# Attention of a second block: probabilities divided before the transposes, values stationary on halves of TensorE's columns

## The chip, the cores and the metric

The kernel runs on one core of a Trainium2 chip. The metric is the device time of one execution in microseconds (us). The time before is the median of three runs.

## The reference, cut to what matters

The program computes two transformer blocks on 256 tokens of width 1024; all is f32. The change lies in the second block, which has three attentions, A, B and C, that read one normalised input h:

```python
qk = qk_norm_g[layer]
a_q = _rms(a_q.reshape(bsz, seq, A_HEADS, HEAD_DIM), qk[0])      # 8 heads of 64, one key/value head
y_a = _dsa_attention(a_q, a_k, a_v, i_q, i_k, i_w, rel_a) @ w_branch_a[layer]
y_b = _nsa_attention(b_q, ..., b_gates, ...) @ w_branch_b[layer]  # 8 heads, 2 key/value heads
y_c = _dilated_attention(c_q, c_k, c_v, rel_c) @ w_branch_c[layer]  # 3 groups of 4 heads
x = x + (g[:, :, 0] * y_a + g[:, :, 1] * y_b + g[:, :, 2] * y_c) @ w_out[layer]
```

Each is a softmax over the keys, p = e / sum(e), and then o = p @ v. A keeps the 64 best keys per query. B adds three results under gates: over 15 compressed keys, over selected blocks and over a window,

```python
o = gb[..., 0:1] * oc + gb[..., 1:2] * osel + gb[..., 2:3] * ow
```

C has three groups of heads; their outputs are weighted by a softmax over the groups' log sums, which is one softmax over the three groups' logits together. With 256 tokens the selected blocks and windows of B and C cover all earlier keys that their masks leave.

## The kernel before, in words

Tokens go in two tiles t of 128. In tile t the keys 0 to 128 (t + 1) count, so t = 0 has one key tile kt and t = 1 has two. The weight products of the program (projections, gates, branches; `mm3`, lines 78 to 80) split both operands into a high and a low part (hi by ScalarE, line 70; lo by VectorE, line 71) and run three fp32r matmuls. The products inside the attentions, other than the scores, are plain f32 matmuls.

One call of `attend` (A and B) handles four heads that share keys and values. `pair_scores` gives the scores of two heads at a time into an "s" bank; `logits` adds bias and mask and finds the row minimum (the scores are negated) on VectorE; `weigh` takes the exponential on ScalarE in place in `lg` with the row sum into `mx`; then, for each key tile, four transposes by TensorE into a "tp" bank (line 1095) and one copy to `pT` by VectorE (line 1096). The values follow head by head (line 1099): the transposed weights of one head (128 keys x 128 queries) are stationary, the 64 columns of values move, and the output, queries on partitions, lands in another "tp" bank:

```python
for i, (c, v) in enumerate(vs):
    for kt in range(t + 1):
        pe.matmul(po[:, c:c + 64], pT[kt][:, i, :], v(kt), ...)
```

Behind that VectorE multiplies the output by one over the row sum (in B also by the gate, and adds it to `oB`): lines 1230, 1338 and 1340, in C line 1375. `split_oT` transposes the finished output (128 queries x 512, in C x 256) in tiles of 128 columns by TensorE (line 1120) and splits it into `oTh` (ScalarE, line 1123) and `oTl` (VectorE, line 1124), which the branch's product needs. A has two attends per token tile, B the compressed part (lines 1311 to 1328) and four attends, C two rounds `jp`, each with two heads of three groups (`weigh` with `joint`).

PSUM has eight banks: four "mm" (projections, gates, branches), two "tp" (transposes and outputs), two "s" (scores). `lg` has two buffers, `mx` and `pT` three.

Instructions are ordered at build time by the tile framework's planner: it runs the program in a model of the engines, and each engine takes, of what is ready, what comes first in the program; a buffer is given out when its first writer is ready. So work that stands later in the program fills gaps: while A's attention runs, the projection `P1` (line 1233); beside B's and C's, `gates(1)` and `gates(2)`. `behind(ins)` queues an instruction behind another one of the same engine, without a wait for its end. Weight units (`wunit`) go through three buffers in fixed turn, so a unit is loaded and split when the third before it has been used up.

Line 1258 is the one place before that puts 64 stationary columns alternately on the two halves of PE's columns (`X[par * 64:(par + 1) * 64, ...]`): 16 f32 matmuls with 64 moving columns.

Of the kernel before, what the change touches and what calls it, by code (L numbers as in the profile page):

```python
# [10 lines left out]
F32 = mybir.dt.float32  # L11
F32R = mybir.dt.float32r
AF = mybir.ActivationFunctionType
ALU = mybir.AluOpType
# [17 lines left out]
def tile_net(ctx: ExitStack, tc: tile.TileContext, I: dict, out: bass.AP):  # L32
# [9 lines left out]
    def bank():  # L42
        return ps.tile([128, 512], F32, tag="mm", name="mm", bufs=4)

    def tbank():
        return ps.tile([128, 512], F32, tag="tp", name="tp", bufs=2)
# [914 lines left out]
    with tc.tile_pool(name="b2", bufs=1, reuse_waits="tile") as b2:  # L961
# [43 lines left out]
        def t512(nm):  # L1005
            return b2.tile([128, 512], F32, tag="t512", name=nm, bufs=3)
# [69 lines left out]
            for j, i in enumerate(at):  # L1076
                ve.tensor_tensor_reduce(lg[:, i, :nk], S[:, j, :], W[j], 1.0, 3e38, ALU.add, ALU.min, mx[:, i:i + 1])

        def weigh(t, n, lg, mx, joint, po, vs):


            nk = 128 * (t + 1)
            if joint:
                ve.tensor_reduce(mx[:, 4:5], mx[:, 0:n], axis=AX.X, op=ALU.min)
                se.activation(lg[:, 0:n, :nk], lg[:, 0:n, :nk], AF.Exp, bias=mx[:, 4:5], scale=-1.0,
                              accum_out=mx[:, 12:13])
            else:
                for i in range(n):
                    se.activation(lg[:, i, :nk], lg[:, i, :nk], AF.Exp, bias=mx[:, i:i + 1], scale=-1.0,
                                  accum_out=mx[:, 12 + i:13 + i])  # L1090
            pT = [b2.tile([128, 4, 128], F32, tag="pT", name="pT", bufs=3) for _ in range(t + 1)]
            for kt in range(t + 1):
                b = tbank()
                for i in range(n):
                    pe.transpose(b[:, i * 128:(i + 1) * 128], lg[:, i, kt * 128:(kt + 1) * 128], ident)  # L1095
                ve.tensor_copy(pT[kt][:, :n, :], b[:, :n * 128].rearrange("p (n c) -> p n c", n=n))
            for i, (c, v) in enumerate(vs):
                for kt in range(t + 1):
                    pe.matmul(po[:, c:c + 64], pT[kt][:, i, :], v(kt),  # L1099
                              start=kt == 0 and (not joint or i == 0), stop=kt == t and (not joint or i == n - 1))  # L1100
            return mx[:, 12:13] if joint else mx[:, 12:12 + n]

        def soft_tiles():
            return (b2.tile([128, 4, 256], F32, tag="lg", name="lg", bufs=2),
                    b2.tile([128, 16], F32, tag="mx", name="mx", bufs=3))

        def attend(t, q, g, kz, W, po, v):


            nk = 128 * (t + 1)  # L1110
            lg, mx = soft_tiles()
            Ss = [pair_scores(t, q, 2 * g + i, kz, nk) for i in range(2)]
            for i in range(2):
                logits(nk, Ss[i], [W(2 * i), W(2 * i + 1)], lg, mx, (2 * i, 2 * i + 1))
            return weigh(t, 4, lg, mx, False, po, [(64 * i, v) for i in range(4)])

        def split_oT(o_t, nb, oTh, oTl, t):
            b = tbank()
            for i in range(nb):
                pe.transpose(b[:, i * 128:(i + 1) * 128], o_t[:, i * 128:(i + 1) * 128], ident)  # L1120
            bv = b[:, :nb * 128].rearrange("p (n c) -> p n c", n=nb)
            tk = slice(t * 128, (t + 1) * 128)
            se.copy(oTh[:, :nb, tk], bv)
            ve.tensor_sub(oTl[:, :nb, tk], bv, oTh[:, :nb, tk].bitcast(F32))
# [90 lines left out]
        oTh, oTl = oT_tiles()  # L1215
        for t in range(2):
            nk = 128 * (t + 1)
            oA = t512("oA")
            for hg in range(2):
                if t == 0:  # L1220
                    Wm = t2k("W0").rearrange("p (h k) -> p h k", h=4)
                    wv = WA[hg][:, :, 128:256]
                else:
                    Wm = wv = WA[hg]
                ve.tensor_add(Wm, wv, madd[t][:, None, :nk].to_broadcast([128, 4, nk]))
                po = tbank()
                den = attend(t, qT, hg, 1, lambda i: Wm[:, i, :nk], po, lambda kt: vA[:, kt, :])
                rden = b2.tile([128, 4], F32, tag="rden", name="rden", bufs=2)
                ve.reciprocal(rden, den)
                ve.tensor_mul(oA[:, hg * 256:(hg + 1) * 256].rearrange("p (h c) -> p h c", c=64),  # L1230
                              po[:, :256].rearrange("p (h c) -> p h c", c=64), rden[:, :, None].to_broadcast([128, 4, 64]))
            split_oT(oA, 4, oTh, oTl, t)
        gA_ = gates(0, *seq["ix"])
        P1 = project(1476, 384)
        branch(0, I["w_branch_a_2"][0], 4, oTh, oTl, gA_)
# [66 lines left out]
        for t in range(2):  # L1302
            tk = slice(t * 128, (t + 1) * 128)
            nk = 128 * (t + 1)
            oB = b2.tile([128, 512], F32, tag="so", name="oB", bufs=2).rearrange("p (h c) -> p h c", c=64)
            co = b2.tile([128, 5, 8], F32, tag="co", name="co", bufs=2)

            Sc = sbank()[:, 0:128].rearrange("p (r h n) -> p r h n", r=4, h=2)
            for pr in range(4):
                for i, (a, c) in enumerate(((0, 0), (1, 0), (0, 1))):  # L1310
                    pe.matmul(Sc[:, pr], qT[:, pr, a, tk], kcZ[:, pr // 2, c], start=i == 0, stop=i == 2)
            pcb = b2.tile([128, 8, 16], F32, tag="pc", name="pc", bufs=1)
            ve.tensor_add(pcb, Sc.rearrange("p r h n -> p (r h) n"), nmask[:, t, None, 0:16].to_broadcast([128, 8, 16]))
            ve.tensor_reduce(co[:, 0, :], pcb, axis=AX.X, op=ALU.min)
            ve.tensor_sub(pcb, pcb, co[:, 0, :, None].to_broadcast([128, 8, 16]))
            se.activation(pcb, pcb, AF.Exp, scale=-1.0)
            ve.tensor_reduce(co[:, 1, :], pcb, axis=AX.X, op=ALU.add)
            ve.tensor_scalar(co[:, 1, :], co[:, 1, :], 1e-30, None, op0=ALU.max)
            ve.reciprocal(co[:, 2, :], co[:, 1, :])
            ve.scalar_tensor_tensor(co[:, 2, :], bgv[:, t, :, 0], nmask[:, t, 16:17], co[:, 2, :],  # L1320
                                    op0=ALU.mult, op1=ALU.mult)
            b = tbank()
            pe.transpose(b[:, 0:128], pcb.rearrange("p h n -> p (h n)"), ident)
            pcT = b2.tile([128, 128], F32, tag="pcT", name="pcT", bufs=1)
            se.copy(pcT, b[:, 0:128])
            po = tbank()
            pe.matmul(po, pcT, vbd.rearrange("p h c -> p (h c)"), start=True, stop=True)
            ve.tensor_mul(oB, po.rearrange("p (h c) -> p h c", c=64), co[:, 2, :, None].to_broadcast([128, 8, 64]))
            for br in range(2):
                for g in range(2):  # L1330
                    po = tbank()
                    den = attend(t, qT, g, 2 * br + g, lambda i: WB[g][:, i, 256 - nk:256], po,
                                 lambda kt: vB[:, kt, 2 * br + g, :])
                    cc = co[:, 3 + br, 4 * g:4 * g + 4]
                    ve.reciprocal(cc, den)
                    ve.tensor_mul(cc, cc, bgv[:, t, 4 * g:4 * g + 4, 1 + br])
                    tmp = t512("ot")[:, :256].rearrange("p (h c) -> p h c", c=64)
                    ve.tensor_mul(tmp, po[:, :256].rearrange("p (h c) -> p h c", c=64),
                                  cc[:, :, None].to_broadcast([128, 4, 64]))
                    ve.tensor_add(oB[:, 4 * g:4 * g + 4, :], oB[:, 4 * g:4 * g + 4, :], tmp)  # L1340
            split_oT(oB.rearrange("p h c -> p (h c)"), 4, oTh, oTl, t)
        gB_ = gates(1)
        branch(1, I["w_branch_b_2"][0], 4, oTh, oTl, gB_)

# [14 lines left out]
        oTh, oTl = oT_tiles()  # L1359
        for t in range(2):  # L1360
            nk = 128 * (t + 1)
            oC = t512("oC")
            for jp in range(2):
                soft = [soft_tiles() for _ in range(2)]
                for g in range(3):
                    S = pair_scores(t, qT, 2 * g + jp, 2 * g + jp, nk)
                    for i in range(2):
                        logits(nk, S[:, i:i + 1], [WC[g][:, 2 * jp + i, 256 - nk:256]], *soft[i], (g,))
                for i in range(2):
                    j = 2 * jp + i  # L1370
                    po = tbank()
                    den = weigh(t, 3, *soft[i], True, po, [(0, lambda kt, h=4 * g + j: vC[:, kt, h, :]) for g in range(3)])
                    rden = b2.tile([128, 4], F32, tag="rden", name="rden", bufs=2)
                    ve.reciprocal(rden[:, 0:1], den)
                    ve.tensor_scalar_mul(oC[:, j * 64:(j + 1) * 64], po[:, 0:64], rden[:, 0:1])
            split_oT(oC, 2, oTh, oTl, t)
        gC_ = gates(2)
        yT = h_tiles()
        branch(2, I["w_branch_c_2"][0], 2, oTh, oTl, gC_, yT)
# [107 lines left out]
```

## Time and profile before

| | us |
|---|---|
| median of 3 runs (1150.12 to 1151.07) | 1150.55 |
| the profiled execution | 1151.18 |
| its span, first to last instruction | 1149.4 |
| PE busy (share of the span) | 1131.6 (98%) |
| VectorE (DVE) busy | 831.6 (72%) |
| ScalarE (ACT) busy | 575.3 (50%) |

PE is TensorE's matmuls, PEld its loads of stationary operands, which overlap with them. A busy instruction is one that is somewhere between its start and its modelled end; matmuls are pipelined, so busy time counts latency too. The stages are, from the span's start: A's attention 702.9 to 727.1 us, B's 778.9 to 818.4, C's 884.6 to 920.9. TensorE's granted clock is 1.00 (2.4 GHz) in all three.

### The profile page before, as it was taken

What the parts mean: (1) busy time and instruction counts of PE and PEld (TensorE: products, weight loads), DVE (VectorE), ACT (ScalarE), POOL (GpSimd) and SP (SyncE); (2) the same over time, 40 slices, a digit from 0 to 9 for tenths busy, and PEclk for the clock granted to TensorE, in tenths of its full rate; (3) what the DMA queues carried; (4) which work ended last, traced back from release to release, by engine and by line L of the source; (5) the groups of instructions that cost most, each with busy time, mean ns of one, the idle gap of its engine ahead of it and who ended that gap; (6) DMA issues with size and microseconds to landing.
All of it is one profiled execution on the core that took longest, in us unless ns stands there. A gap on an engine that the chain in (4) does not pass through costs nothing.

```text
span 1149.4 us, 19941 instructions
## 1 busy us (share of the span) xinstructions
PE 1131.6 (98%) x8007; PEld 1040.1 (90%) x8007; DVE 831.6 (72%) x1547; ACT 575.3 (50%) x1017; POOL 84.1 (7%) x154
## 2 busy tenths in 40 slices
PE   8999999999999999999999999999999999999998
PEld 6989988889999877999988889989999989999986
DVE  5798896889878778766754789788788674655541
ACT  5654444475444436654544665355356356545430
POOL 0111110101121111100000111000100000000000
PEclk9999999999999999999999999999999999999999
DMA  9985554749997993867664283750556254664630
GB/s 310 302 265 160 184 185 141 219 153 336 313 329 284 354 315 106 267 204 254 212 213 137 83 257 114 202 175 28 147 166 221 87 178 139 220 202 166 218 111 37
DMA packets 149098, 229.69 MB, mean 200 GB/s; under 512 B 5708, under 2 KB 121051, under 8 KB 149006
## 3 DMA queue, kind: packets, MB, share of 16 engines
q1 hardware_dynamic: 133986, 176.54, 47.1%
q0 software_dynamic: 14672, 50.63, 13.3%
q8 instruction: 63, 1.03, 0.4%
q10 hardware_dynamic: 348, 1.26, 0.3%
q14 instruction: 29, 0.24, 0.1%
HBM read 226.36 MB, written 2.04 MB: 199 GB/s over the span
## 4 chain that ended last, share of the span: by engine, by line
PE 90%; DVE 7%; ACT 2%; issue 1%; DMA 0%; SPq 0%; DVEq 0%; ACTq 0%
PE mm L80 25%; PE mm L78 25%; PE mm L79 25%; PE tp L1099 2%; DVE wlo L71 2%; PE s L1071 2%; PE s L712 2%; PE tp L736 1%; PE tp L1095 1%; PE s L138 1%; PE s L543 1%; PE tp L723 1%; PE s L542 1%; PE mm L890 1%; PE s L145 1%
## 5 line engine op out<-in xcount | busy, mean ns | idle before, releaser
L71 DVE TENSOR_TENSOR wlo<-raw,whi 128x1024 fp32r<-128x1024 f32 (+2 forms) x316 | 370.7, 1193 | 136.3 <-ACT whi L70 135.8
L70 ACT CAST whi<-raw 128x1024 fp32r<-128x1024 f32 (+2 forms) x316 | 314.6, 1029 | 231.0 <-PE mm L79 95.6
L78 PE MATMUL mm<-hTh,whi 128*128 128x256 f32 x1056 | 297.9, 282 | 0.0
L80 PE MATMUL mm<-hTh,wlo 128*128 128x256 f32 x1056 | 297.6, 282 | 0.0
L79 PE MATMUL mm<-hTl,whi 128*128 128x256 f32 x1056 | 297.1, 281 | 0.0
L79 PEld LDWEIGHTS mm<-hTl,whi 128*128 128x128 f32 x1056 | 199.0, 188 | 0.3
L78 PEld LDWEIGHTS mm<-hTh,whi 128*128 128x128 f32 x1056 | 198.9, 188 | 0.3
L80 PEld LDWEIGHTS mm<-hTh,wlo 128*128 128x128 f32 x1056 | 198.9, 188 | 0.1
L78 PE MATMUL mm<-whi,hTh 128*128 128x256 f32 (+4 forms) x592 | 186.0, 315 | 2.6 <-DVE hTh L336 2.2
L80 PE MATMUL mm<-whi,hTl 128*128 128x256 f32 (+4 forms) x592 | 185.3, 314 | 0.4 <-DVE hTl L337 0.4
L79 PE MATMUL mm<-wlo,hTh 128*128 128x256 f32 (+4 forms) x592 | 184.3, 312 | 0.3 <-DVE wlo L71 0.2
L78 PEld LDWEIGHTS mm<-whi,hTh 128*128 128x128 f32 x592 | 112.2, 189 | 8.8 <-DVE hTh L336 3.1
L80 PEld LDWEIGHTS mm<-whi,hTl 128*128 128x128 f32 x592 | 111.4, 189 | 5.4 <-DVE hTl L337 1.1
L79 PEld LDWEIGHTS mm<-wlo,hTh 128*128 128x128 f32 x592 | 111.9, 189 | 4.3 <-DVE wlo L71 0.7
L132 DVE SCALAR_TENSOR_TENSOR acc<-mraw,csil,acc 128x1024 f32<-128x1024 f32 x80 | 102.1, 1280 | 6.4 <-DMA mraw<-in_w_mod_dram 3.4
L79 PE MATMUL mm<-wlo,hid 128*128 128x512 f32 x264 | 104.2, 395 | 0.0
L78 PE MATMUL mm<-whi,hid 128*128 128x512 f32 x264 | 104.1, 394 | 0.0
L80 PE MATMUL mm<-whi,hid 128*128 128x512 f32 x264 | 103.6, 392 | 0.0
L131 POOL DMA_DIRECT2D mraw<-in_w_mod_dram x80 | 42.8, 535 | 343.9 <-DVE acc L132 235.1
L80 PEld LDWEIGHTS mm<-whi,hid 128*128 128x128 f32 x264 | 49.6, 188 | 12.0 <-issue 1.0
L79 PEld LDWEIGHTS mm<-wlo,hid 128*128 128x128 f32 x264 | 49.6, 188 | 11.6 <-issue 1.0
L78 PEld LDWEIGHTS mm<-whi,hid 128*128 128x128 f32 x264 | 49.6, 188 | 10.9 <-ACT whi L70 0.5
(331 smaller groups left out, 1568.5 us busy)
## 6 DMA issues: line engine op xcount, KB each, us to landing
raw<-in_ffn_w_in_dram SPq DMA_DIRECT2D x44, 1024.0 KB, 7.9
mraw<-in_w_mod_dram POOLq DMA_DIRECT2D x80, 512.0 KB, 5.1
raw<-in_ffn_w_out_dram SPq DMA_DIRECT2D x22, 1024.0 KB, 4.9
raw<-in_w_ffn_in_dram SPq DMA_DIRECT2D x22, 1024.0 KB, 5.2
raw<-in_w_in_dram SPq DMA_DIRECT2D x16, 1024.0 KB, 7.4
raw<-in_w_ffn_out_dram SPq DMA_DIRECT2D x11, 1024.0 KB, 5.0
raw<-in_w_in_dram SPq DMA_DIRECT2D x14, 768.0 KB, 4.4
raw<-in_attn_w_qkv_dram SPq DMA_DIRECT2D x9, 1024.0 KB, 8.9
```

Of the source, the lines that this page charges most:

```text
L70: se.copy(hv[:, sl], raw[:, sl])
L71: seq["sub"] = ve.tensor_sub(lv[:, sl], raw[:, sl], hv[:, sl].bitcast(F32)).ins
L78: pe.matmul(o, lh, rh, start=first, stop=False, **kw)
L79: pe.matmul(o, lh, rl, start=False, stop=False, **kw)
L80: return pe.matmul(o, ll, rh, start=False, stop=last, **kw).ins
L131: gp.dma_start(raw, wv[:, k, g * 1024:(g + 1) * 1024])
L132: ve.scalar_tensor_tensor(acc, raw, csil[:, k, 0:1], acc, op0=ALU.mult, op1=ALU.add)
L138: pe.matmul(b[:, j:j + 1], acc[:, j * 128:(j + 1) * 128], ones[:, 0:1], start=True, stop=True)
L145: mods["mm"] = pe.matmul(b, ones, acc[:, n * 512:(n + 1) * 512], start=True, stop=True).ins
L712: last = pe.matmul(Sm[m], q[p, h, tk], k[p, h, :], start=i == 0, stop=i == 2).ins,
L1071: pe.matmul(S, q[:, pr, a, tk], KZ[:, kz, b, :, :nk], start=i == 0, stop=i == 2)
L1099: pe.matmul(po[:, c:c + 64], pT[kt][:, i, :], v(kt), start=kt == 0 and (not joint or i == 0), stop=kt == t and (not joint or i == n - 1))
```

## The change

The exponentials are divided by their row sum (in B multiplied by the gate as well) on ScalarE, in place in `lg`, ahead of the transposes; in the compressed part VectorE does it on `pcb`. The values then become the stationary operand, 64 columns, and the transposed weights move: two heads side by side (256 columns) for one half of the output's partitions, the two other heads for the other half. The output comes out transposed, and everything that belongs to one token tile is summed in one "mm" bank `O`: in B the compressed part and all four attends. `split_oT` reads `O` directly. The division, the addition and the transposes of the outputs go away. The matmuls on halves are chained by `behind`, so that they stay in the order in which they are written. In `weights_T` the heads are laid out so that heads 0 and 2 stand side by side, then 1 and 3.

```diff
-            for i, (c, v) in enumerate(vs):
-                for kt in range(t + 1):
-                    pe.matmul(po[:, c:c + 64], pT[kt][:, i, :], v(kt), ...)
+        def weights_T(t, kt, n, lg):
+            b = tbank()
+            for i in range(n):
+                j = i % 2 * 2 + i // 2 if n == 4 else i
+                pe.transpose(b[:, j * 128:(j + 1) * 128], lg[:, i, kt * 128:(kt + 1) * 128], ident)
+            pT = b2.tile([128, 4, 128], F32, tag="pT", name="pT", bufs=3)
+            ve.tensor_copy(pT[:, :n, :], b[:, :n * 128].rearrange("p (n c) -> p n c", n=n))
+            return pT
+
+        def halves(O, c, first, last, vps):
+            for half, (v, w) in enumerate(vps):
+                with behind(*seq.get("halves", ())):
+                    i = pe.matmul(O[half * 64:(half + 1) * 64, c], v, w, start=first, stop=last, skip_group_check=True)
+                seq["halves"] = i.ins,
 ...
+            for i in range(4):                                     # attend, behind the exponentials
+                se.activation(lg[:, i, :nk], lg[:, i, :nk], AF.Exp, bias=mx[:, i:i + 1], scale=-1.0, ...)
+            ve.reciprocal(mx[:, 8:12], mx[:, 12:16])
+            if gate is not None:
+                ve.tensor_mul(mx[:, 8:12], mx[:, 8:12], gate)
+            for i in range(4):
+                se.activation(lg[:, i, :nk], lg[:, i, :nk], AF.Copy, scale=mx[:, 8 + i:9 + i])
+            pT = [weights_T(t, kt, 4, lg) for kt in range(t + 1)]
+            for kt in range(t + 1):
+                halves(O, slice(g * 256, (g + 1) * 256), first and kt == 0, last and kt == t,
+                       [(v(kt), pT[kt][:, 2 * i:2 * i + 2, :]) for i in range(2)])
 ...
-            for i in range(nb):                                    # split_oT
-                pe.transpose(b[:, i * 128:(i + 1) * 128], o_t[:, i * 128:(i + 1) * 128], ident)
 ...
+            ve.tensor_mul(pcb, pcb, co[:, 2, :, None].to_broadcast([128, 8, 16]))     # B, compressed part
-            pe.matmul(po, pcT, vbd.rearrange("p h c -> p (h c)"), start=True, stop=True)
-            ve.tensor_mul(oB, po..., co[:, 2, :, None].to_broadcast([128, 8, 64]))
+            for pr in range(4):
+                pe.matmul(O[:, pr * 128:(pr + 1) * 128], vbd[:, 2 * pr:2 * pr + 2, :]..., pcT, ...)
 ...
+                for lg, mx in soft:                                # C
+                    ve.tensor_reduce(mx[:, 4:5], mx[:, 0:3], axis=AX.X, op=ALU.min)
+                    se.activation(lg[:, 0:3, :nk], lg[:, 0:3, :nk], AF.Exp, bias=mx[:, 4:5], scale=-1.0, ...)
+                    ve.reciprocal(mx[:, 8:9], mx[:, 12:13])
+                    se.activation(lg[:, 0:3, :nk], lg[:, 0:3, :nk], AF.Copy, scale=mx[:, 8:9])
+                for kt in range(t + 1):
+                    pT = [weights_T(t, kt, 3, lg) for lg, _ in soft]
+                    for g in range(3):
+                        halves(O, slice(jp * 128, (jp + 1) * 128), jp + kt + g == 0, ...,
+                               [(vC[:, kt, 4 * g + 2 * jp + i, :], pT[i][:, g, :]) for i in range(2)])
```

## Rows read from the trace of the kernel before

**Rows 1.** The page's first part: busy us (share of the span) xinstructions.
```profile
PE 1131.6 (98%) x8007; PEld 1040.1 (90%) x8007; DVE 831.6 (72%) x1547; ACT 575.3 (50%) x1017; POOL 84.1 (7%) x154
```

**Rows 2.** The page's fourth part: the chain that ended last, by engine.
```profile
PE 90%; DVE 7%; ACT 2%; issue 1%; DMA 0%; SPq 0%; DVEq 0%; ACTq 0%
```

**Rows 3.** Windows of A, B, C: us; busy PE, PEld, DVE, ACT, POOL (xinstructions); clock; DMA.
```profile
702.90:727.10 24.20, 23.16 (x179) 20.91 (x178) 20.80 (x64) 15.17 (x45) 4.19 (x8) 1.00 0.49 126
778.90:818.40 39.50, 39.50 (x310) 36.79 (x309) 31.36 (x116) 20.15 (x67) 4.20 (x8) 1.00 0.20 57
884.60:920.90 36.30, 36.30 (x290) 34.63 (x288) 24.56 (x92) 14.49 (x27) 0.00 (x0) 1.00 0.36 132
```

**Rows 4.** Line 1099: ns minimum/median/maximum, first and last start, forms.
```profile
L1099 PE MATMUL tp<-vv,pT x168: 217/275/323, 781.8 to 919.0; 128*128 128x64 f32 x168
```

**Rows 5.** Timeline of PE in B: start, us from first start to last end.
```profile
803.50 1.67 PE L1099 MATMUL tp<-vv,pT 128*128 128x64 f32 x14
805.01 0.50 PE L1095 MATMUL tp<-idsel,lg 128*128 128x128 f32 x3
...
811.04 0.60 PE L1095 MATMUL tp<-idsel,lg 128*128 128x128 f32 x4
```

**Rows 6.** Timeline of PE: B's compressed product and the transposes behind it.
```profile
779.42 1.02 PE L1327 MATMUL tp<-vbd,pcT 128*128 128x512 f32 x2
780.28 0.60 PE L1095 MATMUL tp<-idsel,lg 128*128 128x128 f32 x4
```

**Rows 7.** Timeline of PE, windows 722.1 to 722.3, then 722.3 to 722.5.
```profile
722.12 0.39 PE L1258 MATMUL s<-small,vv 128*64 128x64 f32 x6
...
722.12 0.57 PE L1258 MATMUL s<-small,vv 128*64 128x64 f32 x12
```

**Rows 8.** Timeline of PE: transposes, a run on halves, transposes.
```profile
724.52 0.39 PE L1120 MATMUL tp<-idsel,oA 128*128 128x128 f32 x2
724.84 0.57 PE L1258 MATMUL s<-small,vv 128*64 128x64 f32 x12
725.34 0.44 PE L1120 MATMUL tp<-idsel,oA 128*128 128x128 f32 x2
```

**Rows 9.** Groups by line and form, ScalarE, B's window: busy us, mean ns | idle before.
```profile
L1089 ACT ACTIVATE lg<-lg,mx 128x256 f32<-128x256 f32 x16 | 8.0, 502 | 6.4 <-DVE mx L1077 6.1
...
L1089 ACT ACTIVATE lg<-lg,mx 128x128 f32<-128x128 f32 x12 | 4.7, 393 | 0.4 <-DVE mx L1077 0.4
L70 ACT CAST whi<-raw 128x1024 fp32r<-128x1024 f32 x4 | 4.2, 1042 | 2.8 <-PE mm L79 1.5 <-issue 1.4
...
L1325 ACT COPY pcT<-tp 128x128 f32<-128x128 f32 x2 | 0.5, 267 | 0.8 <-PE tp L1323 0.8
```

**Rows 10.** Line 303, a scaled copy: ns minimum/median/maximum.
```profile
L303 ACT ACTIVATE z<-x,nc x8: 706/714/727, 642.9 to 962.4; 128x512 f32<-128x512 f32 x8
```

**Rows 11.** Line 1338, the division in B: ns minimum/median/maximum.
```profile
L1338 DVE TENSOR_TENSOR ot<-tp,co x8: 424/425/425, 783.0 to 814.6; 128x256 f32<-128x256 f32 x8
```

**Rows 12.** Timelines of VectorE and ScalarE in B: copies, last exponential, cast, last subtraction.
```profile
801.83 1.29 DVE L1096 COPY pT<-tp 128x512 f32<-128x512 f32 x2
...
809.54 0.49 ACT L1089 ACTIVATE lg<-lg,mx 128x256 f32<-128x256 f32 x1
809.94 0.19 ACT L1089 ACTIVATION_READ_ACCUMULATOR lg<-lg,mx 128x1 f32 x1
...
817.08 0.59 ACT L1123 CAST oTh<-tp 128x512 fp32r<-128x512 f32 x1 [5.53 <-PE tp L1120]
...
817.70 0.69 DVE L1124 TENSOR_TENSOR oTl<-tp,oTh 128x512 fp32r<-128x512 f32 x1 [1.19 <-ACT oTh L1123]
```

**Rows 13.** Timeline of PE: branch a's first products; idle before in brackets.
```profile
726.45 0.50 PE L78 MATMUL mm<-oTh,whi 128*128 128x256 f32 x2 [0.42 <-ACT oTh L1123]
```

**Rows 14.** Timelines at C's end: VectorE's last subtraction; PE's first product of branch c.
```profile
920.44 0.43 DVE L1124 TENSOR_TENSOR oTl<-tp,oTh 128x256 fp32r<-128x256 f32 x1 [0.83 <-ACT oTh L1123]
...
927.12 0.28 PE L78 MATMUL mm<-oTh,whi 128*128 128x256 f32 x1
```

More of the change, by code (lines that the diff above doesn't have):

```diff
@@ L1077, in logits @@
                 ve.tensor_tensor_reduce(lg[:, i, :nk], S[:, j, :], W[j], 1.0, 3e38, ALU.add, ALU.min, mx[:, i:i + 1])
[L1079 to L1091, printed above, removed]
-            for kt in range(t + 1):
[L1093 to L1096, printed above, removed]
-            for i, (c, v) in enumerate(vs):
[L1098 to L1101, printed above, removed]
+        def weights_T(t, kt, n, lg):
[11 more added lines that the diff above has]
+                seq["halves"] = i.ins,
         def soft_tiles():
@@ L1105, in soft_tiles, with attend @@
                     b2.tile([128, 16], F32, tag="mx", name="mx", bufs=3))
-        def attend(t, q, g, kz, W, po, v):
+        def attend(t, q, g, kz, W, O, v, first, last, gate=None):
             nk = 128 * (t + 1)
@@ L1114, in attend, with split_oT @@
                 logits(nk, Ss[i], [W(2 * i), W(2 * i + 1)], lg, mx, (2 * i, 2 * i + 1))
-            return weigh(t, 4, lg, mx, False, po, [(64 * i, v) for i in range(4)])
-        def split_oT(o_t, nb, oTh, oTl, t):
-            b = tbank()
-            for i in range(nb):
-                pe.transpose(b[:, i * 128:(i + 1) * 128], o_t[:, i * 128:(i + 1) * 128], ident)
-            bv = b[:, :nb * 128].rearrange("p (n c) -> p n c", n=nb)
+            for i in range(4):
+                se.activation(lg[:, i, :nk], lg[:, i, :nk], AF.Exp, bias=mx[:, i:i + 1], scale=-1.0,
+                              accum_out=mx[:, 12 + i:13 + i])
+            ve.reciprocal(mx[:, 8:12], mx[:, 12:16])
[7 more added lines that the diff above has]
+                       [(v(kt), pT[kt][:, 2 * i:2 * i + 2, :]) for i in range(2)])
+        def split_oT(O, nb, oTh, oTl, t):
+            bv = O[:, :nb * 128].rearrange("p (n c) -> p n c", n=nb)
             tk = slice(t * 128, (t + 1) * 128)
@@ L1217, in tile_net @@
             nk = 128 * (t + 1)
-            oA = t512("oA")
+            O = bank()
             for hg in range(2):
@@ L1225, in tile_net @@
                 ve.tensor_add(Wm, wv, madd[t][:, None, :nk].to_broadcast([128, 4, nk]))
[L1226 to L1232, printed above, removed]
+                attend(t, qT, hg, 1, lambda i: Wm[:, i, :nk], O, lambda kt: vA[:, kt, :], hg == 0, hg == 1)
+            split_oT(O, 4, oTh, oTl, t)
         gA_ = gates(0, *seq["ix"])
@@ L1304, in tile_net @@
             nk = 128 * (t + 1)
-            oB = b2.tile([128, 512], F32, tag="so", name="oB", bufs=2).rearrange("p (h c) -> p h c", c=64)
             co = b2.tile([128, 5, 8], F32, tag="co", name="co", bufs=2)
@@ L1325, in tile_net @@
             se.copy(pcT, b[:, 0:128])
-            po = tbank()
-            pe.matmul(po, pcT, vbd.rearrange("p h c -> p (h c)"), start=True, stop=True)
-            ve.tensor_mul(oB, po.rearrange("p (h c) -> p h c", c=64), co[:, 2, :, None].to_broadcast([128, 8, 64]))
+            O = bank()
+            for pr in range(4):
+                pe.matmul(O[:, pr * 128:(pr + 1) * 128], vbd[:, 2 * pr:2 * pr + 2, :].rearrange("p h c -> p (h c)"), pcT,
+                          start=pr == 0, stop=False, skip_group_check=True)
             for br in range(2):
                 for g in range(2):
[L1331 to L1341, printed above, removed]
+                    attend(t, qT, g, 2 * br + g, lambda i: WB[g][:, i, 256 - nk:256], O,
+                           lambda kt: vB[:, kt, 2 * br + g, :], False, br == 1 and g == 1,
+                           bgv[:, t, 4 * g:4 * g + 4, 1 + br])
+            split_oT(O, 4, oTh, oTl, t)
         gB_ = gates(1)
@@ L1361, in tile_net @@
             nk = 128 * (t + 1)
-            oC = t512("oC")
+            O = bank()
             for jp in range(2):
@@ L1368, in tile_net @@
                         logits(nk, S[:, i:i + 1], [WC[g][:, 2 * jp + i, 256 - nk:256]], *soft[i], (g,))
[L1369 to L1376, printed above, removed]
+                for lg, mx in soft:
+                    ve.tensor_reduce(mx[:, 4:5], mx[:, 0:3], axis=AX.X, op=ALU.min)
+                    se.activation(lg[:, 0:3, :nk], lg[:, 0:3, :nk], AF.Exp, bias=mx[:, 4:5], scale=-1.0,
+                                  accum_out=mx[:, 12:13])
+                    ve.reciprocal(mx[:, 8:9], mx[:, 12:13])
[3 more added lines that the diff above has]
+                    for g in range(3):
+                        halves(O, slice(jp * 128, (jp + 1) * 128), jp + kt + g == 0, jp == 1 and kt == t and g == 2,
+                               [(vC[:, kt, 4 * g + 2 * jp + i, :], pT[i][:, g, :]) for i in range(2)])
+            split_oT(O, 2, oTh, oTl, t)
         gC_ = gates(2)
```

## The prediction

> **What bounds the kernel now.** I read the page's first part, then the chain of waits, then the three attention stages as windows, then the timeline of each. TensorE is busy for 98% of the span [rows 1] and holds 90% of the chain that ended last [rows 2]. A busy PE says little by itself, since its instructions overlap, so the windows count more: in B's and C's attention PE is never idle (39.50 of 39.50 us, 36.30 of 36.30), in A's it lacks 1 us [rows 3]. Beside the attention's own matmuls PE runs fillers there: the next projections and gates (lines 78 to 80). So the price of a PE instruction is its share of the stream, not its duration of some 275 ns; I take prices from how far apart the starts or the ends of a run of equal instructions lie. A saved PE instruction is a gain only while fillers last; where they run out, the attention's chain sets the end.
>
> **The value products.** An f32 matmul is two passes in the trace: the 84 value matmuls of B and C give 168 records [rows 4], so A's 24 give 48. Before, the 128x128 weights are stationary and 64 value columns move. Fourteen such passes take 1.51 us to the next instruction's start, 0.108 us each [rows 5]; 216 of them are 23.3 us. An attend with one key tile (t = 0) costs 8 x 0.108 = 0.86, with two (t = 1) 1.73; in C a pair of heads costs 12 x 0.108 = 1.30 per key tile.
>
> After, 64 value columns are stationary and 256 columns of weights move (128 in C), one product on each half of PE's columns. The moving price: two f32 passes of 512 columns take 0.86 us [rows 6], so 0.43 per 512 columns, 0.215 per 256, 0.107 per 128. Whether the two halves run at once is shown by the one place that uses halves now, L1258, with 64 moving columns: six passes end at 722.51, twelve at 722.69 [rows 7], so 0.03 us a pass, 0.06 per pair; one pass of 64 columns alone should move for 0.43 / 8 = 0.054. Two halves at once cost what one does. I take the same for 256 and 128 columns: a pair of matmuls (two passes each) costs 0.43, in C 0.215.
>
> The price of going in and out: the transposes before a run on halves end at 724.91, the run's twelve passes at 725.41. That is 0.50 for six pairs of 0.06 (0.35), so 0.15 lost on entry. The two transposes behind it end at 725.78, 0.37 later instead of 2 x 0.11, so 0.15 lost on leaving [rows 8]. Each uninterrupted run on halves pays 0.30 us. The Trainium skill, TensorEngine Tiling (Array Packing), Key Properties, says that changing the tiling mode drains TensorE; the trace agrees with these two 0.15s. Its Theoretical Speedup table promises up to 2x for a dimension of 64, and by that alone the value products would lose half of 23.3 us, 11.7. By row and rule together most of this goes to the drains.
>
> How many runs there are the planner decides. With t = 0 there is one pair per attend: 0.43 + 0.30 = 0.73 against 0.86, 6 x 0.13 = 0.8 us. With t = 1 the two pairs wait for two copies by VectorE, 1.29 us for both [rows 12], so the second pair is ready some 0.6 later than the first, and a filler may go between. In one run: 0.86 + 0.30 = 1.16 against 1.73, 6 x 0.57 = 3.4; in two runs 1.46, 6 x 0.27 = 1.6. I take the middle, 2.5. In C one run per key tile is 0.645 + 0.30 = 0.95 against 1.30, six times 0.35 = 2.1; but the first head's copy comes half a us before the second's, so the first product may go alone (0.215 + 0.30, then 0.645 + 0.30, 1.46 in all), which loses 6 x 0.16 = 1.0. I take a gain of 0.5, below the middle, because the chained order makes every later product wait for the second head.
>
> **Other work on PE.** The output transposes of split_oT go, four per token tile in A and B and two in C, 20 in all; three transposes in a row last 0.50, four 0.60 [rows 5], so some 0.11 each: 2.2 us. The compressed branch replaces four passes of 512 columns (1.72) by 16 passes of 128 with a full stationary (0.107 by columns moved, 0.108 by the loads of L1099): 1.7, no change. PE's sum: 0.8 + 2.5 + 0.5 + 2.2 = 6.0 us less, bounds 3.6 and 8.5; by stage A 1.9, B 3.1, C 0.9.
>
> **ScalarE and VectorE.** ScalarE gets 48 scalings in A and B and 8 in C. The nearest row is a copy with a scale per partition, SBUF to SBUF, of 128x512: 0.71 [rows 10]. The exponentials of 128x128 and 128x256 take 0.39 and 0.50 [rows 9], 0.11 per 128 columns; carried on to 512 that is 0.72, the same line. So I take 0.39, 0.50, and for C's 384 and 768 columns 0.61 and 0.93. The lower end is a plain copy of 128x128 out of PSUM, 0.27 [rows 9], 0.12 below. Neighbours overlap by some 0.09 (the exponential from 809.54 and its reading, 0.40 to the next start [rows 12]), so in B 16 x 0.30 + 16 x 0.41 = 11.4 us come on top of 20.15 busy of 39.50 [rows 3]: 31.5, or 87% of a 36 us stage (lower end 27.7). That is no bound, but the nearest to one beside PE. VectorE loses twelve divisions of 256 columns (0.42 each [rows 11]) and B's eight additions of the same width, 8.4 us, besides C's eight short divisions and two wide ones; it gains two multiplies of 128 columns.
>
> **What is late next.** In B the last exponential ends at 810.03 and the last subtraction at 818.39 [rows 12], a tail of 8.4 us: copies, values, division, an addition, transposes, cast, subtraction. After: reciprocal and gate 0.3 (two instructions of four columns, an estimate), four scalings 1.7, transposes 0.45, two copies 1.3, last pair with its entry 0.6, cast 0.59, subtraction 0.69 [rows 12]: 5.6. So the tail shortens by 2.8 us although a step is put into it. Ahead of it each attend keeps ScalarE longer, 1.2 us with t = 0 and 1.6 with t = 1, against 0.84 less on VectorE and 0.13 to 0.57 less on PE. The branch's products start right as the chain ends, and the gates are used up there: what PE saves beyond the chain's gain becomes idle time. I book 1.7 of 3.1, a little over the middle between nothing and all. In A PE already waits 0.42 us for the cast at 726.45 [rows 13] with no filler left but L1258; its tail loses a product, a division and transposes (2 us) and gains reciprocal and scalings (1.9). I book 1.0 of 1.9. In C the chain ends at 920.87 and gates last until 927.12 [rows 14]: 6 us of cover for a chain through two weight buffers that grows by about 1 us for each of four pairs of heads. I book all of 0.9; without the cover that growth would cost up to 4 us.
>
> The accumulator O takes one of four "mm" banks through a whole token tile; fillers need two (projection) or one (gate), so three are enough, and the "tp" banks are free of outputs. No DMA is added or moved; SP and GpSimd issue the same transfers in the same order.
>
> **The sum.** 1.0 + 1.7 + 0.9 = 3.6 us. The profiled execution took 1151.18 us (span 1149.4), so 1147.6; the median of the runs shown is 0.6 lower, so 1147.0.
>
> **Rivals.**
> *The halves do not overlap with wide operands* (slower). L1258 moves 64 columns; nothing shows two streams of 256. Then a pair costs 0.86 (C 0.43): with drains t = 0 loses 0.30 x 6, t = 1 0.29 to 0.59 x 6, C 0.29 to 0.59 x 6, less 2.2 for the transposes: 3.0 to 6.6 us more, 1153.6 to 1157.2. For it: 256 columns are four times the tested width. Against: the 64-column pairs run with no loss at all. Full overlap is worth 18 x 0.43 + 18 x 0.215 = 11.6 us, so it turns slower once half of that is lost. Chance 0.10.
> *ScalarE's longer chain takes the place.* If scalings land behind weight casts of 1.04 us [rows 9], the chains of A and B stay as long as before, fillers run out, and only C's 0.9 is left: 1149.7; each chain that grows by one or two such casts adds as much, up to 1154. For it: ScalarE at 87% in B. Against: the shorter tail, and 8 us less on VectorE. Chance 0.28, of which 0.08 ends above 1152.8.
> *The drains are hidden, or the runs are long.* If the planner puts several pairs into one run, PE saves 8.5 us, without any drain 13.9: 1136.7 to 1142, the chains shortening with it. For it: the price of the drains rests on one run. Against: both drains are there, and the chains must follow. Chance 0.12.
>
> **How the numbers follow.** The forecast case has 0.50; its own range is 1143 to 1149.5 (all of PE's saving at its upper middle, or hardly any of A's and B's). Faster by over 0.2% (2.3 us, about what a measurement can tell) means below 1148.2: 0.12 and 0.42 of the 0.50, 0.54. Within 0.2%: 0.08 + 0.20 = 0.28. Slower: 0.10 + 0.08 = 0.18. The range 1140 to 1153 leaves out some 0.06 below and 0.14 above.
>
> **What would show it.** In the changed profile: passes on halves with 256 columns start in pairs a few ns apart, two pairs in 0.43 us (right) or 0.86 (wrong); the instruction ahead of and behind each run ends 0.15 us later than its kind does; A and B have 12 runs or 18; the output transposes are gone and the cast follows the halves directly; ScalarE's scalings last 0.39 and 0.50. PE idle ahead of branches a and b, released by ScalarE or VectorE, speaks for the second rival; PE's own work down by 12 us for the third; a stage C that ends after its gates would make the 0.9 wrong.

## The result: 4% slower, and the profile after

The changed kernel takes 1196.59 us (median of 4, 1195.29 to 1199.18) against 1150.81 of the kernel before on the same chip: ratio 1.040 [1.0387, 1.0413]. The forecast was 1147.0, the range 1140 to 1153. The profiled execution took 1197.72, its span 1195.9.

The page's first part and its chain, after (they answer to [rows 1, 2]):

```profile
PE 1143.4 (96%) x7927; PEld 1032.6 (86%) x7927; DVE 824.0 (69%) x1519; ACT 598.1 (50%) x1073; POOL 84.4 (7%) x154
...
PE 87%; DVE 8%; ACT 3%; issue 1%; DMA 1%; SPq 0%; DVEq 0%; ACTq 0%
```

PE issues 80 instructions fewer, and yet it is busy for 11.8 us more. To find where, cut the program at marks that both kernels have: from the end of A's query projection to branch a's first product, from the end of branch a to branch b, from the end of branch b to branch c. Windows (columns as in [rows 3]), before:

```profile
677.76:726.45 48.69, 47.48 (x385) 45.06 (x383) 45.23 (x139) 27.06 (x60) 4.19 (x8) 1.00 0.52 151
738.12:818.40 80.28, 79.84 (x602) 73.62 (x600) 66.25 (x211) 42.86 (x113) 4.20 (x8) 1.00 0.39 120
829.51:927.12 97.61, 96.59 (x653) 93.73 (x652) 73.11 (x196) 47.96 (x77) 0.00 (x0) 1.00 0.47 153
```

and after:

```profile
675.52:747.25 71.73, 52.52 (x320) 44.88 (x321) 44.36 (x134) 30.64 (x72) 4.20 (x8) 0.79 0.31 96
758.29:852.92 94.63, 85.35 (x590) 71.25 (x588) 60.36 (x195) 54.11 (x145) 4.20 (x8) 0.93 0.33 103
863.98:973.64 109.66, 101.54 (x649) 92.32 (x648) 71.77 (x188) 53.66 (x85) 0.00 (x0) 0.95 0.42 136
```

The stages grow by 23.0, 14.4 and 12.1 us, 49.4 together; the whole span grows by 46.5, so 2.9 come back elsewhere. Window less PE busy is PE's idle time: 2.7 us before, 36.6 after, 33.9 more. The other 15.5 is PE busy for longer with 80 instructions fewer, at a granted clock of 0.79, 0.93 and 0.95; how much of it the clock takes isn't parted here (the eighth experiment does it for A). As shares of the windows, DVE falls from 93, 83 and 75% to 62, 64 and 65%, and ACT goes from 56, 53 and 49% to 43, 57 and 49%: no other engine became the bound. In the PE timeline of A's stage, after (start, us; idle before, with its releaser, in brackets):

```profile
675.12 0.40 PE L80 MATMUL mm<-whi,hTl 128*128 128x512 f32 x1
685.88 1.94 PE L1023 MATMUL tp<-idsel,qn 128*128 128x128 f32 x8 [10.36 <-DVE qn L1050]
...
695.88 4.92 PE L1071 MATMUL s<-KZ,qT 128*128 128x256 f32 x12 [6.24 <-DVE mx L1077]
...
709.19 1.12 PE L1095 MATMUL mm<-pT,vA 128*64 128x256 f32 x4 [0.67 <-DVE pT L1087]
710.24 0.58 PE L78 MATMUL mm<-hTh,whi 128*128 128x256 f32 x1
```

For 10.36 and 6.24 us PE waits for VectorE, which works on A's top-k and norms. VectorE was as busy in this stretch before; then `gates(0)` kept PE working beside it. The first 14 us, before and after:

```profile
676.00:690.00 14.00, 13.67 (x109) 13.15 (x108) 13.94 (x38) 8.85 (x12) 0.00 (x0) 1.00 0.60 197
...
676.00:690.00 14.00, 3.76 (x14) 2.99 (x14) 13.93 (x49) 3.29 (x5) 0.00 (x0) 0.57 0.47 159
```

Now the gates' first product comes at 710.24, right behind a value product into `O` of the second token tile. Its weights were split long before, in VectorE's timeline:

```profile
679.27 1.22 DVE L71 TENSOR_TENSOR wlo<-raw,whi 128x1024 fp32r<-128x1024 f32 x1
...
680.49 1.22 DVE L71 TENSOR_TENSOR wlo<-raw,whi 128x1024 fp32r<-128x1024 f32 x1
```

So the gates wait for something else, and what they share with `O` is the ring of "mm" banks: the four buffers that all tiles of that name take in turn.

### The profile page after: what moved, and what is told of

Same layout as the page of the kernel before. It is cut to its first block, busy times and chain, and to the rows that moved or that the text cites. A ratio compares the mean times of both kernels' runs of the same rounds, so it can differ in the third digit from the quotient of the medians.

```text
span 1195.9 us, 19817 instructions
## 1 busy us (share of the span) xinstructions
PE 1143.4 (96%) x7927; PEld 1032.6 (86%) x7927; DVE 824.0 (69%) x1519; ACT 598.1 (50%) x1073; POOL 84.4 (7%) x154
## 4 chain that ended last, share of the span: by engine, by line
PE 87%; DVE 8%; ACT 3%; issue 1%; DMA 1%; SPq 0%; DVEq 0%; ACTq 0%
PE mm L80 24%; PE mm L78 24%; PE mm L79 24%; DVE wlo L71 2%; PE s L1071 2%; PE mm L1095 2%; PE s L712 2%; PE tp L1085 1%; PE tp L736 1%; PE s L138 1%; DMA raw<-in_w_mod_dram 1%; PE tp L723 1%; PE mm L890 1%; PE s L145 1%; PE s L543 1%
## 5 line engine op out<-in xcount | busy, mean ns | idle before, releaser
L71 DVE TENSOR_TENSOR wlo<-raw,whi 128x1024 fp32r<-128x1024 f32 (+2 forms) x316 | 370.7, 1193 | 165.8 <-ACT whi L70 165.3
```

The costliest lines, as they stand in the source:

```text
L71: seq["sub"] = ve.tensor_sub(lv[:, sl], raw[:, sl], hv[:, sl].bitcast(F32)).ins
```

## The experiments

My theory: the planner gives the banks of one ring to tiles in the order in which the tiles' first writers stand in the program. `O` of t = 0 and of t = 1 stand ahead of the gates' tiles and are first written by value products, late in the stage; so no gate or projection can have a bank earlier, however many are free. Rivals: a bank held through a token tile leaves too few; ScalarE's scalings; the low clock; the `behind` chain. The last has no run of its own, but the others answer it: the first, third and ninth experiments keep the chain, and the hole closes; the second has no chain, and the hole opens.

**1. O from another ring.**

```diff
-            O = bank()
+            O = tbank()        # "tp"; created just ahead of the first value product
```

> The changed kernel, with one difference: the accumulator O of a token tile comes from the two "tp" banks instead of the four "mm" banks, so that the transposes keep one bank. Theory (place in the ring): the planner hands out the "mm" banks in program order of the tiles' first writers; O0 and O1 stand ahead of the gates' tiles and are first written by value products late in the stage, so gates and projections cannot start before. With O out of that ring the gates fill the top-k stretch again: PE idle between 676 and 700 us falls from some 16 us to under 3, branch a starts near 726 instead of 747, total 1142 to 1152 us. Rival (ScalarE's scalings lengthen the chain): nothing changes for the chain, and transposes with one bank are slower, so 1190 to 1205. Rival (low clock by the halves themselves): halves stay, so 1190 or more.

Measured: 1152.39, ratio 1.0014 [1.0004, 1.0024]. From 1196.6 that is 44 us back. Windows of the top-k stretch:

```profile
676.00:690.00 14.00, 13.67 (x113) 13.27 (x112) 13.91 (x37) 8.81 (x11) 0.00 (x0) 1.00 0.60 191
690.00:700.00 10.00, 10.00 (x87) 10.00 (x86) 10.00 (x37) 3.57 (x6) 0.00 (x0) 1.00 0.53 182
```

PE idles 0.33 us there. Branch a starts at 725.27, as expected; halves and scalings are still in. What remains is a loss of 0.1%, just past the upper edge of what the theory gave: see 5 and 6.

**2. The kernel before, with its value outputs in the "mm" ring.**

```diff
-                po = tbank()   # A, B and C
+                po = bank()
```

> The kernel before (no halves, no scaling, outputs transposed as before), with one difference: the outputs of the value products take "mm" banks instead of "tp" banks, each only for the short time until VectorE has read it. Theory (place in the ring): these tiles stand ahead of the gates' tiles in the program, so the gates wait for the last attend of each stage: PE stands idle in the top-k stretch as in the changed kernel, total 1185 to 1215 us. Rival (a bank held through a token tile is what costs): each is held for some 2 us only, so under 1155. Rival (ScalarE or halves): neither is in this kernel, so 1151.

Measured: 1207.4, ratio 1.0485 [1.0467, 1.0503]. The same hole opens in a kernel without halves, without scalings and with short-lived outputs (PE timeline):

```profile
687.17 1.94 PE L1023 MATMUL tp<-idsel,qn 128*128 128x128 f32 x8 [10.36 <-DVE qn L1050]
...
697.18 1.62 PE L1071 MATMUL s<-KZ,qT 128*128 128x256 f32 x6 [6.25 <-DVE mx L1077]
...
711.86 0.43 PE L1099 MATMUL mm<-vA,pT 128*128 128x64 f32 x2 [0.57 <-DVE pT L1096]
712.13 0.39 PE L1120 MATMUL tp<-idsel,oA 128*128 128x128 f32 x2
712.28 0.37 PE L78 MATMUL mm<-hTh,whi 128*128 128x256 f32 x1
```

The gates begin as soon as the last attend's output has its bank (711.86, 712.28). Order alone is enough.

**3. O stays where it is; the gates move ahead of it in the program.**

```diff
+        with tc.high_priority(offset=-300):      # negative: later in priority, earlier in the ring
+            gA_ = gates(0, range(4), None, ...)  # B, C: two gates ahead, one between the tiles t
         for t in range(2):
             O = bank()
```

> The changed kernel, O still in "mm" banks and held through the token tile; only the place in the program moves: the gates of A stand ahead of its attention, its projection between the token tiles, of B's and C's gates two ahead, one between the token tiles, one behind; their priority is lowered by an offset so that they stay fillers. Theory (place in the ring): gates take their banks before O0 and O1, PE idle between 676 and 700 us under 3 us, total 1140 to 1155. Rival (a bank held through a token tile leaves too few): still one bank short, 1180 to 1200. Rival (ScalarE's scalings): 1190 or more.

Measured: 1157.72, ratio 1.006 [1.0043, 1.0077]: 39 us back with the bank still held, 2.7 above the upper end of what the theory gave. The lowered priority put the end of one gate of C behind branch c, and the next product (with `w_out`) waited for that gate:

```profile
936.79 0.79 PE L78 MATMUL mm<-whi,hTh 128*128 128x512 f32 x1 [3.70 <-ACT gate L1140]
```

**4. The kernel before, with a bank held and nobody blocked.**

```diff
+        H = bank()
+        pe.transpose(H[:, 0:128], ident, ident)   # ready at once
         ...                                       # the attention
+        ve.tensor_add(<unused>, H[:, 0:4], <last split output>)
```

> The kernel before, with one more "mm" bank taken through the whole attention of A, B and C: a tile written at once by one transpose of the identity ahead of the attention and read (four columns, into an unused tile) behind the last output's split. Its place in the ring blocks nobody, since its first writer is ready. Theory (place in the ring): three banks are enough, at most 3 us more, 1150 to 1154. Rival (a bank held is what costs): 1180 to 1200.

Measured: 1155.67, ratio 1.0047 [1.0029, 1.0064], 3.3 to 7.4 us more. A held bank costs about a tenth of what the change lost, though more than the 3 us I gave it. PE's timeline names one place: the second gate of A waits until ScalarE has read the first one out of its bank (line 1136), while the query projection still has two banks and `H` one.

```profile
684.81 0.58 PE L78 MATMUL mm<-hTh,whi 128*128 128x256 f32 x1 [2.93 <-ACT gate L1136]
```

**5 and 6. A and B changed alone, C changed alone** (O from "tp" as in 1).

```diff
-            oC = t512("oC")                 # 5 keeps this code of before in C alone,
+            O = tbank()                     # 6 changes C alone
```

> Attentions A and B as changed, with O from the "tp" banks (as in the first experiment), attention C as before. Theory: with the place in the ring mended, A gains 1.2 us (branch a starts at 725.27 instead of 726.45) and B 0.7 (branch b 816.56 instead of 818.40), and what the first experiment gives back (branch c 927.34 against 927.12) is C's own: so this kernel ends 1.8 us before the kernel before, 1147.8 to 1149.2. Rival (the gain is given back anyway, because the units of weights behind B arrive at their own time): branch c starts at 927 whatever C does, 1150 to 1151.

> The complement: only attention C is changed, with O from the "tp" banks; A and B as before. Theory (C's chain grows by some 7 us, from an end at 920.9 to one past the gates, which end at 927.1): the cover of 6 us is used up, branch c starts 2 us later and runs 0.8 us longer, 1152.5 to 1154. Rival (C's loss in the first experiment came from what A and B did to the weight units): 1150 to 1151.

Measured: 1151.17, 1.0006 [0.9998, 1.0015], and 1153.39, 1.0027 [1.0018, 1.0036]. The sixth came out as expected: C loses. The fifth did not: no gain can be told. By windows A and B do gain (fifth: 48.28 and 79.59 against 48.69 and 80.28 before), but the profiled execution gives it back in branch a, where the clock falls after two gaps of 0.7 us in A's tail (the first ends with VectorE's copy of the weights, the second with ScalarE's cast):

```profile
715.00:725.90 10.90, 9.09 (x79) 6.19 (x78) 8.76 (x20) 9.07 (x23) 2.10 (x4) 1.00 0.96 248
725.90:732.00 6.10, 5.87 (x35) 5.67 (x36) 3.29 (x13) 0.00 (x0) 0.00 (x0) 0.72 0.50 172
```

Branch a lasts 13.24 us there, 11.66 in the first experiment, which has the same A and B and kept 1.00. So two short gaps ahead of a long product were followed once by a loss larger than themselves, and once by none; what made the difference isn't shown. C's window in the sixth:

```profile
829.07:928.46 99.39, 97.21 (x650) 90.51 (x648) 72.62 (x189) 55.85 (x88) 0.00 (x0) 1.00 0.47 158
```

**7. Scalings alone.** The kernel before; only the division moves, to ScalarE and ahead of the transposes.

```diff
+                ve.reciprocal(mx[:, 8:12], mx[:, 12:16])    # B: times the gate
+                for i in range(n):
+                    se.activation(lg[:, i, :nk], lg[:, i, :nk], AF.Copy, scale=mx[:, 8 + i:9 + i])
-                ve.tensor_mul(oA..., po..., rden...)        # becomes a copy; in B it goes, in C as in A
```

> The kernel before, with one part of the change: the weights are divided on ScalarE ahead of the transposes in A, B and C (B's by the gate too); the values, their outputs in "tp" banks and the outputs' transposes are as before, and the divisions on VectorE become plain copies (A, C) or go (B). It prices ScalarE's scalings alone. Theory (they are no bound): A and B within 1 us, C's chain 4 us longer but covered by 6 us of gates, 1149.5 to 1152. Rival (the scalings alone lengthen C's chain by 7 us): 1152.5 to 1155, branch c later by 2 us or more.

Measured: 1162.09, ratio 1.0094 [1.008, 1.0108]: 11.5 us, more than either theory. Windows of the three stages:

```profile
676.03:728.03 52.00, 48.73 (x385) 45.40 (x383) 48.24 (x153) 32.36 (x76) 4.18 (x8) 0.98 0.59 176
741.70:824.37 82.67, 81.09 (x602) 73.92 (x600) 65.02 (x205) 55.31 (x148) 4.19 (x8) 1.00 0.38 123
837.41:936.41 99.00, 96.95 (x654) 93.83 (x652) 74.22 (x197) 55.74 (x88) 0.00 (x0) 1.00 0.48 160
```

They are 3.3, 2.4 and 1.4 us longer; the branches behind them add 4.3 (13.67, 13.04 and 6.20 against 11.67, 11.11 and 5.81), and a and b begin at a low clock:

```profile
728.00:734.00 6.00, 5.97 (x30) 5.74 (x31) 1.80 (x6) 0.00 (x0) 0.00 (x0) 0.58 0.07 27
824.40:830.00 5.60, 5.60 (x33) 5.41 (x34) 1.02 (x2) 0.00 (x0) 0.00 (x0) 0.70 0.43 143
```

ScalarE's timeline at B's last attend shows the step: the last exponential, then 1.39 us idle for a reciprocal that stands behind two copies on VectorE, then the four scalings.

```profile
814.30 0.49 ACT L1091 ACTIVATE lg<-lg,mx 128x256 f32<-128x256 f32 x1
814.70 0.19 ACT L1091 ACTIVATION_READ_ACCUMULATOR lg<-lg,mx 128x1 f32 x1
816.27 1.70 ACT L1097 ACTIVATE lg<-lg,mx 128x256 f32<-128x256 f32 x4 [1.39 <-DVE mx L1095]
```

From the exponential's end (814.79) to the last scaling's (817.97) it is 3.2 us; the prediction had 2.0. At A's last attend it is 3.8 (718.41 to 722.19): there the scalings stand behind two weight casts on ScalarE itself.

```profile
717.92 0.50 ACT L1091 ACTIVATE lg<-lg,mx 128x256 f32<-128x256 f32 x1
...
718.93 1.65 ACT L70 CAST whi<-raw 128x816 fp32r<-128x816 f32 x2
720.48 1.71 ACT L1097 ACTIVATE lg<-lg,mx 128x256 f32<-128x256 f32 x4
```

**8. Idle time or low clock?** The changed kernel, with useless products in the holes of A.

```diff
+        dm = bank()
+        with tc.high_priority(offset=-1500):
+            for _ in range(72):
+                pe.matmul(dm[:, 0:128], ones, ones, start=True, stop=True)
```

> The changed kernel, with 72 f32 matmuls of ones (128x128, results unused, 0.215 us each at full clock, 15.5 us in all) at the lowest priority behind A's query projection, so that they run where PE is idle; the gates still wait for O1. It parts the idle time from the low clock that follows it (0.57, 0.50, 0.84 and 0.72 in the four stretches from 676 to 720 us). Theory (idle is the larger part): the clock stays at 1.00 and A's part of the loss falls by the 4 to 6 us that work at half speed cost, 1189 to 1193. Rival (the low clock is the larger part): below 1186. Rival (the clock costs nothing on the path): 1196.

Measured: 1197.45 (1193.08 to 1200.39), ratio 1.0406 [1.0385, 1.0427]; the total misses the 1189 to 1193 of the theory and can't be told from the changed kernel's, as the last rival has it. By windows, in the profiled execution, A is 3.7 us shorter than in the changed kernel, at a clock of 0.97, just under the 4 to 6 expected; B and C, whose code is the same, ran at 0.91 and 0.92 instead of 0.93 and 0.95 and took 3.3 longer.

```profile
677.00:745.05 68.05, 62.78 (x464) 56.73 (x464) 44.51 (x134) 30.63 (x72) 4.18 (x8) 0.97 0.32 100
756.53:851.59 95.06, 85.59 (x590) 71.66 (x588) 60.34 (x195) 54.08 (x145) 4.19 (x8) 0.91 0.31 101
862.64:975.17 112.53, 104.68 (x649) 94.26 (x648) 71.87 (x188) 53.66 (x85) 0.00 (x0) 0.92 0.39 133
```

With the clock nearly back, A is still 19.4 us longer than before. So in A the hole is by far the larger part of the loss and the clock the smaller; for B and C it wasn't parted.

**9. The third experiment, ordered.**

```diff
+        gC_ = gates(2, (0, 1), None)             # normal priority; A and B likewise
         for t in range(2):
+            if t == 1: gates(2, (2,), gC_)
+            with tc.high_priority(offset=(294, 270)[t]):   # the attention: earlier in priority
                 O = bank()
```

> As the third experiment (the changed kernel, O in "mm" banks, gates of A ahead of its attention, of B and C two ahead, one between the token tiles, one behind), but ordered so that no gate falls behind the branch that needs it: here the attentions' priority is raised by an offset instead of the gates' lowered. In the third experiment the last quarter of a gate of C ran behind branch c and PE then stood idle for 3.70 us. Theory: that idle time goes, and with two banks for the transposes the tails of A and B have no gap: 1148 to 1152 us. Rival (the held bank and the longer softmax chain cost 5 to 7 us by themselves, as in the fourth experiment): 1153 to 1158.

Measured: 1148.16 against 1149.87, ratio 0.9983 [0.9975, 0.9992]: 0.9 to 2.9 us faster than the kernel before, and 48 faster than the change. The page's first line and the three stages:

```profile
PE 1125.4 (98%) x7927; PEld 1022.7 (89%) x7927; DVE 821.2 (72%) x1519; ACT 596.4 (52%) x1073; POOL 84.1 (7%) x154
```

```profile
676.40:724.29 47.89, 45.15 (x321) 39.36 (x321) 43.31 (x134) 30.55 (x72) 4.18 (x8) 1.00 0.53 153
735.35:815.05 79.70, 78.63 (x590) 67.10 (x588) 59.62 (x195) 53.32 (x145) 4.19 (x8) 1.00 0.39 122
826.52:923.12 96.60, 95.55 (x649) 89.68 (x648) 70.88 (x188) 53.26 (x85) 0.00 (x0) 1.00 0.48 154
```

The program is the change's, with as many instructions (x7927); only places and priorities differ. What this order of the gates would do for the kernel before was not run, so the 0.9 to 2.9 us belong to the change and the order together.

**10 and 11. The scalings on VectorE**, head by head: in the ninth kernel, and in the fifth.

```diff
-                se.activation(lg[:, i, :nk], lg[:, i, :nk], AF.Copy, scale=mx[:, 8 + i:9 + i])
+                ve.reciprocal(mx[:, 8 + i:9 + i], mx[:, 12 + i:13 + i])
+                ve.tensor_scalar(lg[:, i, :nk], lg[:, i, :nk], mx[:, 8 + i:9 + i], ..., op0=ALU.mult, ...)
```

> The kernel of the ninth experiment, with one difference: the weights are divided on VectorE instead of ScalarE, head by head right behind each exponential (a reciprocal of one column and one multiplication with a scalar per partition, in B with the gate as second scalar; in C one multiplication per head). Theory (the scaling step makes the chain longer: alone it cost 11.5 us in the seventh experiment, since all four exponentials come before the first scaling and the four scalings follow one another on ScalarE): the chain gets shorter by about 1.5 us per attend, 2 to 6 us less than the ninth experiment. Rival (VectorE, which casts weights too, becomes the late engine): the same or slower than the ninth experiment.

> The kernel of the fifth experiment (A and B changed, O from the "tp" banks, C as before), with the same difference: A's and B's weights are divided on VectorE, head by head. Theory (as for the tenth): 1.5 to 4 us less than the fifth, 1147 to 1149.7, faster than the kernel before. Rival (VectorE becomes late): 1151 or more.

Measured: 1151.45, 1.0014 [1.0006, 1.0023], and 1158.46, 1.007 [1.0058, 1.0082]: 3 and 7 us slower than with ScalarE, as the rival had it. In A and B of the eleventh PE waits 5.6 us for VectorE's scaled weights and copies, against 1.8 us for its copies in the fifth. For the tenth the place isn't shown: the stretch from 676 to 745 us of its profiled execution ran at a clock of 0.95. VectorE's groups in B's window of the eleventh (busy us, mean ns):

```profile
L1142 DVE TENSOR_SCALAR lg<-lg,mx,bg 128x256 f32<-128x256 f32 x16 | 6.1, 406 | 0.0
...
L1142 DVE TENSOR_SCALAR lg<-lg,mx,bg 128x128 f32<-128x128 f32 x16 | 4.9, 341 | 0.0
...
L1138 DVE RECIPROCAL mx<-mx 128x1 f32<-128x1 f32 x32 | 3.5, 150 | 0.5 <-ACT lg L1135 0.5
```

14.5 us come onto VectorE, and a head costs 0.41 + 0.15 there, against 0.43 on ScalarE (four in 1.70).

## Why the prediction was wrong

**The step that failed** is "The accumulator O takes one of four "mm" banks through a whole token tile; fillers need two (projection) or one (gate), so three are enough". I counted banks and took it, as I had written of the kernel before, that a buffer is given out when its first writer is ready. That is wrong: the tiles of a ring get their banks in program order. The second experiment opens the hole although each output has its bank only briefly, the third and ninth close it although `O` has one throughout: the place in the ring decides, and the number counts for little (5.2 us in the fourth). Whether a tile's place is where it is made or where its first writer stands, no run parts. What the step put at nothing cost most of the 45.8 us: the first experiment, which takes `O` out of the ring, gives 44 back. None of the rivals had it: each looked at an engine's own work, while here PE's filler work was ready and had no bank. The Trainium skill, Perfetto Trace Analysis, Optimization Strategy, says that the same gap repeating on the engine that should be saturated can mean that there isn't enough SBUF or PSUM for the next tile. The trace agrees in part: PE has such gaps (10.36 and 6.24 us in A) and they come from the tiles' buffers, but there were enough of these: the same four banks serve the ninth kernel, whose clock in the three stages is 1.00.

**The rest of the sum**, with that step mended, as the ninth kernel has it:

*Value products.* Halves overlap at 256 columns. In the first experiment's PE timeline from the filler ahead of a pair (782.09; fillers start 0.12 apart) to the transposes behind it is 0.79, so the pair costs 0.67. One half after the other would need 0.86 for the columns alone; with 0.43 for both at once, 0.24 is left for going in and out (booked: 0.30). The first and ninth runs have 17 such pairs behind a filler: 14 cost 0.67 or 0.68, three 0.77 or 0.78.

```profile
782.09 0.28 PE L78 MATMUL mm<-hTh,whi 128*128 128x256 f32 x1
782.29 0.65 PE L1095 MATMUL tp<-pT,vv 128*64 128x256 f32 x4
782.88 0.55 PE L1085 MATMUL tp<-idsel,lg 128*128 128x128 f32 x3
```

The first rival is out. Nor are the drains hidden, as the third had it.

*PE's sum.* Booked 6.0; PE's busy time falls by 6.2 on the page (1131.6 to 1125.4), by 4.6 in the three stages. Busy time counts latency too, so this is near the booked sum and no measure of it.

*What reaches the end.* Booked A 1.0, B 1.7, C 0.9. Stage and branch together, ninth against before: A 0.8 + 0.6 (branch a 11.06 instead of 11.67), B 0.6 - 0.4 (11.47 instead of 11.11), C 1.0 + 0.2 (5.63 instead of 5.81). But 32 passes of B's index product (L1258 of before, L1259 there), which ran in A's tail [rows 8], have moved behind branch a:

```profile
744.65 1.15 PE L1259 MATMUL s<-small,vv 128*64 128x64 f32 x32
```

If they cost PE those 1.15 us in either place (an estimate), A gains 0.3 and B 1.3: A's term was too large, the two others nearer. Together 2.8 of 3.6 in the profiled executions; between the medians the whole gain is 1.7, and the order of the gates has its unknown part in both.

*ScalarE.* The durations were right: four scalings of 256 columns take 1.70, booked 1.7. The waiting in front of them was not: the second rival's mechanism is real (in A the scalings land behind casts; in B they wait for VectorE) and, alone, the scalings cost more than it priced (11.5 us against "up to 1154"), of which 4.3 fall in the branches, two of them with a low clock. In the ninth kernel the halves, the sum in PSUM, the lost transposes and the new order pay it back. By difference that would be a loss of about 11 and a gain of about 13, but no run shows the second alone. So it is partly luck that the ninth kernel comes near the forecast's 1147.0.

*C.* "Without the cover that growth would cost up to 4 us" is what the sixth experiment met: its last gate product starts at 925.45, then PE waits 0.29, 0.87 and 0.58 us for C's chain, and the kernel loses 2.8 us by the medians. In the ninth, with two banks for the transposes and the gates in their new order, C has no such wait and gains; which of the two does it isn't parted.

## What to carry to other kernels

Before a tile moves into a ring that fillers use, write down the order in which the ring's tiles are first written in the program: a tile whose first writer comes late blocks every later tile of the ring, however many buffers are free. If PE loses time and no other engine becomes full, look for work that ran in that hole before and ask what it is waiting for. Price a change that moves a step into a chain by running the step alone; here a step that was booked as paid for cost 11.5 us by itself.

## What the runs showed of the hardware that was not expected

Gaps of 0.72 and 0.69 us ahead of a branch were followed by a granted clock of 0.72 over the next 6 us in one execution (the fifth experiment, shown there), and gaps of 0.73 and 0.69 by 1.00 in another with the same A and B (the first): the branch took 13.24 or 11.66 us. The first experiment's window from branch a's start:

```profile
725.27:731.00 5.73, 5.51 (x46) 5.30 (x47) 3.29 (x13) 0.00 (x0) 0.00 (x0) 1.00 0.54 183
```

In these two executions the price of a short idle time was not fixed.
